# Merge-ring gates and squares, two early buffers, and no address offsets in a one-layer hybrid trunk kernel

## The chip, the cores and the metric

The kernel runs on one core of a Trainium2 chip. The metric is the device time in microseconds (us) of one execution; the time before is the median of three runs, 871.64 us (871.51 to 872.29). In the texts PE is the matrix engine, DVE the vector engine, ACT the scalar engine, POOL the general engine, and SP the engine that only issues transfers. A line number such as L142 is a line of the kernel before.

## The reference

One layer, 512 tokens, 1024 channels, float32. The input is normalised and projected once to 8192 columns, which are split among three token mixers and the gates of three branches:

```python
h = rms_norm(x, norm_mix[l])
proj = jnp.einsum('bsd,dc->bsc', h, w_in[l])
u_pool, u_lru, q, k, v, g_logits = jnp.split(proj, splits, axis=-1)
gates = jax.nn.sigmoid(g_logits + b_gate[l]).reshape(B, S, N_BRANCH, D_MODEL)
y_pool = pool_mixer(u_pool, w_pool[l], pool_scale[l])      # windows 2, 4, 8, 16: mean minus token, 4 maps of 256 x 256
y_lru = rglru_mixer(u_lru, ...)                            # conv of width 4, two gates, decay a, h = a h + b over the tokens
qh, kh = rms_norm(q), rms_norm(k)                          # per head, 8 heads of 128
y_sb = stick_breaking_attention(qh, kh, vh)                # w = sigmoid(z) * prod of (1 - sigmoid) of later keys
merged = sum(gates[:, :, n] * (y_n @ w_branch[n]))         # n = pool, lru, attention
x = x + merged @ w_out
x = x + (silu(h2 @ w_ffn_gate) * (h2 @ w_ffn_up)) @ w_ffn_down     # h2 = rms_norm(x), width 2816
```

## The kernel before

Every large product is made in a split form: each float32 operand is written as a rounded part `hi` and a remainder `lo` (type fp32r), and three matmuls (hi hi, hi lo, lo hi) are accumulated. A weight set of 128 x 1024 is loaded into a tile `raw` or `qw`, ACT copies it to `whi` (L141) and DVE subtracts to `wlo` (L142); 24 or 48 matmuls then use the pair. The pool `wp` holds three of each. The rings are what the text calls sets of equal buffers that tiles take in turn: `mp` has four buffers of 2 x 512 float32 per partition, the ring `b` of the pool `ap0` has 13 of them, and in the attention stage the rings `s` and `l` (`slot`, `slot_ld`) have 30 and 12 buffers of 512 float32. A tile that takes a buffer waits until the last reader of the previous tile in it is done.

The order of the work is set by the program and a planner. The main program walks through weight sets and calls `tick()` between pieces of matmul work; each `tick` emits one entry of a background list (`bg`, and `abg` for attention). Pieces under `tc.high_priority(n)` are moved forward in the order of their engine's queue by the planner, which works with its own costs; the queue that results is fixed when the program is built, and each engine then runs its queue in that order, waiting on semaphores.

The stages, with the times of the profiled execution:

- to about 98 us: `hu`, the scaled input, branch 0's gates (`ps_gate`), the norm, the first LRU chunks `ps_lru`. The matrix engine runs nine warm-up matmuls ahead of the first load.
- about 50 to 130 us: the recurrent mixer, four channel chunks c. `lru_chunk` gives closures: `conv` (L642, L651, twelve steps on DVE, output `xc`), `split` (`xch` L656, `xcl` L657), `gates` (matmuls `lg` L667, then tanh `lr` L671 and `li` L672 on ACT), `tanh` (`li` L676, `lt` L679). Then `lru_exp` (L697, L700), `lru_decay` and `lru_input` (`lt`, `ls`, L705 to L714), and `lru_scan` (L720). Branch 1's gates are computed between these chunks: `gate_store` writes the tanh to `gt` (L609) and a POOL transfer carries it to a scratch tensor.
- about 130 to 290 us: V, K and Q by a seven-product scheme (`ps_q`, L837). A partial result is copied from PSUM by `snap` (`r`, L850) at raised priority, finished by `final` (L854), and `post` makes the squares `sq` (L797) whose sums normalise q and k; `post2` scales K (L816). Then two gate chunks `gx`, `gy`.
- about 290 to 475 us: four pooling chunks (`ps_pool`), then branch 1 of the merge (`ps_br` with `yHH`, `yHL`), then branch 0 (with `yph`, `ypl`). `evac_u` copies a pooling chunk from PSUM (`up`, L983), `pool_mean` makes the window sums on DVE (`pw`, L991, L992, L997) and its split (`p30h`, `p30l` and so on, L941, L942), `pool_back` multiplies by the group's map (`pps`) and writes `yph` (L1010) and `ypl` (L1011). Between half weight sets, a `tick` of `abg` emits the attention pieces of `head_tasks`: loads of q, k, v (`at`, L1052), transposes (`pq`, L1059) and their splits `qkh`, `qkl`, the scores `z`, the scans `E` (L1096), `A` (L1098), transposes of the weights (`pw` on PE, L1109; `wth`, `wtl`), and the output `py`. The PSUM tiles `pq`, `pw`, `py` and `pps` share the three buffers of the pool `paux`; those of `ps_pool` and `ps_br` share the pool `pmm`.
- from about 475 us: branch 2, the output projection and the feed-forward network, with weights split at L1445, L1446 and L1565.

Two things in the tile pools carry no data: `pad`, 41 float32 that shift later tiles of `cst`, and 128 unused columns in each tile of `whi` and `wlo`; a weight tile is the slice that starts at column 0, 4, 8 or 12 (the list `STEPS`, for the first four of some stages) or 16 (`OFF`).

Of the kernel before, what the change touches and what calls it, by code (L numbers as in the profile page):

```python
# [16 lines left out]
P = 128  # L17
# [14 lines left out]
NTICK = (1, 1)  # L32
H = S // 2
AHEAD = 200
PAD = 41


OFF = 16
STEPS = (0, 4, 8, 12)
NAW, NAT, NAB = 8, 8, 13  # L40
NSP = 42
NLD = 12
# [25 lines left out]
def layer_kernel(ctx: ExitStack, tc: tile.TileContext, x, xt, vecs, w_in, w_qkv7, w_gate7, w_pool, w_rg, w_ig,  # L68
# [5 lines left out]
    cst = ctx.enter_context(tc.tile_pool(name="cst", bufs=1))  # L74
    mp = ctx.enter_context(tc.tile_pool(name="mp", bufs=4))
    wp = ctx.enter_context(tc.tile_pool(name="wp", bufs=3))
    late = ctx.enter_context(ExitStack())
    hstack = ctx.enter_context(ExitStack())
    hp = hstack.enter_context(tc.tile_pool(name="hp", bufs=1, side="right"))
# [47 lines left out]
        return [t[:, 0:2, :], t[:, 2:4, :]]  # L127


    def weight_tiles(nh, nl, o=0):  # L130
        return [wp.tile([P, 1024 + 128], F32R, tag=tag, name=n)[:, o:o + 1024]
                for tag, n in (("whi", nh), ("wlo", nl))]

    def split_w(raw, shape, n, o=0):
        hi, lo = weight_tiles("whi" + n, "wlo" + n, o)
        if len(shape) == 3:
            hi, lo = (t.rearrange("p (a b) -> p a b", a=shape[1]) for t in (hi, lo))
        else:
            hi, lo = (t.rearrange("p (a b c) -> p a b c", a=shape[1], b=shape[2]) for t in (hi, lo))
        with tc.high_priority(60):  # L140
            act(hi, raw, AF.Copy)  # L141
            dve.tensor_tensor(lo, raw, hi.bitcast(F32), ALU.subtract)  # L142
        return hi, lo
# [58 lines left out]
    def add_seven(un, nm, i):  # L202
        u, pieces, shape = UNITS[un]
        last = i == pieces - 1

        def make(n):
            if nm == "S4":
                r = qraw[u, "12", i]
                dve.tensor_tensor(r, r, qraw[u, "S2", i], ALU.add)
            src = qraw[u, {"S1": "21", "S3": "11", "S4": "12"}.get(nm, nm), i]  # L210
            o = 0
            if u >= 3:
                o = goffs.pop(0) if goffs else OFF
            parts = split_w(src, [P] + list(shape), n, o)
            if nm == "11":
                qraw[u, "S2", i] = r = b4(list(shape), f"qs{u}{i}")
                dve.tensor_tensor(r, qraw[u, "21", i], src, ALU.add)
                add = nc.gpsimd.dma_start(src, seven_src(u, "21", i), accum_op=ALU.add)
            if last:
                if un < 3:  # L220
                    seven_load(un + 1, {"S1": ("21",), "S3": ("11",), "S4": ("12",), "22": ("22",)}.get(nm, ()))
                elif un == 3 and nm == "11":
                    with tc.issue_after(add.ins):
                        seven_load(un + 1, ("21", "11"))
                elif un == 3:
                    seven_load(un + 1, {"12": ("12",), "S2": ("22",)}.get(nm, ()))
            return parts
        specs.append((("seven", u, nm, i), make))

    goffs = list(STEPS)  # L230

    def add_then(f):
        specs[-1] = (specs[-1][0], lambda n, make=specs[-1][1]: (make(n), f())[0])
# [24 lines left out]
              (0, "S4"), (1, "S2"), (0, "22"), (1, "12"), (1, "S4"), (1, "S3"), (1, "22"))  # L258
    BY, BX = {}, {}
    BNEXT = {"11": ("21", BY), "S1": ("11", BX), "S2": ("12", BX)}  # L260
    boffs = list(STEPS)

    def bsrc(u, nm):
        return w_br7[u, CH[nm], KH[nm]]
# [1 line left out]
    def add_branch7(u, nm):  # L266
        def make(n):
            if nm in ("12", "22"):
                t = wp.tile([P, 2, 4, P], F32, tag="raw", name="raw" + n)
                nc.sync.dma_start(t, bsrc(u, nm))  # L270
            else:
                t = (BY if nm in ("11", "S3") else BX)[u]
            parts = split_w(t, [P, 2, 4, P], n, boffs.pop(0) if boffs else OFF)
            if nm in BNEXT:
                m, buf = BNEXT[nm]
                nc.gpsimd.dma_start(buf[u], bsrc(u, m), accum_op=ALU.add)
            return parts
        specs.append((("b7", u, nm), make))
# [51 lines left out]
        return vt[:, o:o + 1]  # L330


    cst.tile([P, PAD], F32, tag="pad", name="pad")
    warm = cst.tile([P, S], BF16, tag="warm", name="warm")
    dve.memset(warm, 1.0)
    idn = cst.tile([P, P], F32, tag="idn", name="idn")
    make_identity(nc, idn)
# [106 lines left out]
    with ExitStack() as first:  # L444
# [10 lines left out]

        wps = pb.tile([P, 2, S], F32, tag="mm", name="warm_ps")
        for i in range(WARM):
            nc.tensor.matmul(wps[:, 0, :], warm[:, 0:P], warm, start=True, stop=True)

# [137 lines left out]


        def gate_store(br, c, pss, scaled):
            gt = b4([2, S], f"gt{br}{c}")
            for j in range(2):
                o = two(gt[:, j, :])
                g = in_order(pss[j])
                if not scaled:
                    dve.tensor_tensor(o, g, two(rb), ALU.mult)
                    g = o
                act(o, g, AF.Tanh, scale=0.5, bias=bhalf[:, 8 * br + 2 * c + j:8 * br + 2 * c + j + 1])  # L609
            nc.gpsimd.dma_start(gd[br, c].rearrange("(j p) t -> p j t", p=P), gt)  # L610
# [141 lines left out]
        pss.append(chan_chunk(("gate", 0, 3), hu, 2, pb))  # L752
        gate_store(0, 3, pss[3], False)
        tick(len(bg))

        def gate1(c):
            gate_store(1, c, chan_chunk(("gate", 1, c), hn, 1, pb), True)
# [21 lines left out]
        gate1(2)  # L779
        for f, c in ((lru_decay, 2), (lru_decay, 3), (lru_input, 2)):  # L780
            step(of(f, c))
        bg.extend(prepare_t())
        gate1(3)


# [6 lines left out]

        def post(t, i, j, r):
            if t < 2:
                sq = b4([2, 512], f"sq{t}{i}{j}")
                if t == 0:
                    act(sq, r, AF.Square)  # L797
                    dve.tensor_reduce(qss[:, 2 * j:2 * j + 2, 4 * i:4 * i + 4],
                                      sq.rearrange("p a (b d) -> p a b d", d=HD), AX.X, ALU.add)
                    store(t, i, j, r)  # L800
                    return
                s_ = cst.tile([P, 8], F32, tag="ssq", name=f"ssq{t}{i}{j}", bufs=2)
                act(sq, r, AF.Square)
# [88 lines left out]
            nc.gpsimd.dma_start(gd2[cc, j], t)  # L892

        for cc in range(2):
            tx, ty = b4([2, S], f"gx{cc}"), b4([2, S], f"gy{cc}")
            if cc:

                dve.memset(pb.tile([P, 2, S], F32, tag="mm", name="skip_g")[:, 0, 0:1], 0.0)
# [46 lines left out]
    with ExitStack() as mix:  # L945
# [32 lines left out]
                dve.tensor_tensor(lo, r, hi.bitcast(F32), ALU.subtract)  # L978
                pool_w[2 * h + g] = (hi, lo)

        def evac_u(ps, name):
            u = slot(name)
            act(two(u), in_order(ps), AF.Copy)  # L983
            return u

        def pool_mean(g, j, u):
# [32 lines left out]

        def pool_chunk(g):  # L1020
            pss = chan_chunk(("pool", g), hn, 1)
            us = [evac_u(pss[j], f"up{g}{j}") for j in range(2)]
            for j in range(2):
                bg.append(lambda j=j, u=us[j]: pool_mean(g, j, u))
            if g != POOL[0]:
                queue_pool_back(POOL[POOL.index(g) - 1])
# [17 lines left out]
        def head_tasks(h):  # L1044
# [3 lines left out]

            def load():
                for t in range(3):  # L1050
                    r = slot_ld(f"at{h}{t}", (NS, HD))
                    nc.sync.dma_start(r, qd[t, g][:, hd].rearrange("(b p) c -> p b c", p=P))  # L1052
                    st["raw", t] = r

            def trans():
# [117 lines left out]
        def queue_attention():  # L1173
# [8 lines left out]
            for p in range(max(todo) + 1):  # L1182
                abg.append(lambda fs=todo.get(p, ()): [f() for f in fs])

        load_pool_weights(0)
        queue_attention()
        for g in POOL:
            pool_chunk(g)
        queue_pool_back(POOL[3])
# [108 lines left out]
    with ExitStack() as ffn:  # L1298
# [112 lines left out]
        raw = {}  # L1411
        A = {}
        made = [0, NDIRECT]
        offs = []

        def load_a(c):
            for nm in ("11", "21", "22", "12"):
# [11 lines left out]
        def make_a(upto):  # L1429
            while made[0] < min(upto, len(steps)):  # L1430
                c, nm = steps[made[0]]
                made[0] += 1
                if (c, nm) == (NDIRECT, "11"):
                    offs.extend(STEPS)
                while made[1] < min(c + 2, DOWN):
                    load_a(made[1])
                    made[1] += 1
                sums_a(c, nm)
                A[c, nm] = split_a(raw[c, nm], f"{c}_{nm}")

        def split_a(src, n):
            o = offs.pop(0) if offs else OFF
            h, l = (t.rearrange("p (w k c) -> p w k c", w=2, k=4)
                    for t in weight_tiles("wh" + n, "wl" + n, o))
# [134 lines left out]
        def make_d(upto):  # L1579
            while dmade[0] < min(upto, len(dsets)):  # L1580
                nm, n = dsets[dmade[0]]
                dmade[0] += 1
                if dmade[0] == 1:
                    offs.extend(STEPS)
# [157 lines left out]
```

## Time and profile before

| | us |
|---|---|
| median of three runs | 871.64 |
| profiled execution | 872.32 |
| its span | 870.5 |
| PE busy | 860.6 |
| DVE busy | 741.1 |
| ACT busy | 523.1 |
| POOL busy | 91.2 |

The span is what the profiler's records cover; 1.8 us of the profiled execution lie around it. A row of the timeline has the start, the duration, the engine, the line, the operation, output and inputs with their shapes, and in brackets the idle time ahead of it with what ended it. Durations of neighbours on DVE and ACT overlap by about 0.1 us, so that the distance of two starts says what one instruction costs its queue (a split on DVE: 1.22 long, 1.14 from start to start).

### The profile page before, as it was taken

Reading aid. Unit: us, or ns where it says so; the run is one execution under the profiler, and the core shown is the slowest. Engines: PE = TensorE matmul, PEld = TensorE weight load, DVE = VectorE, ACT = ScalarE, POOL = GpSimd, SP = SyncE. Lnnn points to the kernel's source line nnn. Section 1 sums busy time; section 2 is a strip of 40 time slices with the busy share of each in tenths; the row PEclk is TensorE's granted clock in tenths of the full one; section 3 lists DMA queues with packets and bytes.
Section 4 is the critical chain, followed back from the end, with each engine's and each line's share of the span. In section 5 each row is a group of like instructions: output and inputs, shape, how many; then the busy total and the mean of one; then the engine's idle time right before and its main releaser. Section 6 shows DMA issues by size and latency. Waiting matters only on the chain.

```text
span 870.5 us, 14271 instructions
## 1 busy us (share of the span) xinstructions
PE 860.6 (99%) x5563; PEld 790.0 (91%) x5563; DVE 741.1 (85%) x961; ACT 523.1 (60%) x727; POOL 91.2 (10%) x130
## 2 busy tenths in 40 slices
PE   9999999999999999999999999999999999999998
PEld 7888878888899888889889998889999999999998
DVE  7899897998796599977988786699998888899974
ACT  7554989557966565565665545464555555755642
POOL 1110002232433101000001100000000000121200
PEclk9999999999999999999999999999999999999999
DMA  9586356798582886644636955345543433797913
GB/s 339 165 287 203 98 167 187 212 324 253 178 275 73 241 243 203 221 122 151 214 103 167 199 172 169 98 139 151 156 111 97 116 104 119 228 240 194 196 42 121
DMA packets 116643, 154.08 MB, mean 177 GB/s; under 512 B 8160, under 2 KB 90080, under 8 KB 116576
## 3 DMA queue, kind: packets, MB, share of 16 engines
q1 hardware_dynamic: 103904, 107.30, 38.4%
q0 software_dynamic: 12528, 45.62, 22.0%
q8 instruction: 43, 0.70, 0.3%
q10 hardware_dynamic: 144, 0.26, 0.1%
q14 instruction: 24, 0.20, 0.1%
HBM read 132.71 MB, written 18.87 MB: 174 GB/s over the span
## 4 chain that ended last, share of the span: by engine, by line
PE 84%; DVE 7%; ACT 5%; DMA 2%; issue 1%; SPq 0%; ACTq 0%; DVEq 0%
PE ps_y L321 11%; PE ps_x L321 8%; PE ps_q L837 7%; PE ps_dy L1661 6%; PE ps_dx L1661 5%; PE ps_br L312 3%; PE ps_br L313 3%; PE ps_br L314 3%; PE ps_bY L1280 2%; PE ps_gate L740 2%; PE ps_gy L321 2%; DVE wlo L142 2%; PE ps_bX L1280 2%; PE ps_gx L321 2%; PE ps_lru L312 1%; PE ps_out L312 1%
## 5 line engine op out<-in xcount | busy, mean ns | idle before, releaser
L141 ACT ACTIVATE whi<-raw 128x1024 fp32r<-128x1024 f32 x69 | 72.9, 1056 | 78.3 <-PE ps_out L313 16.1
L142 DVE TENSOR_TENSOR wlo<-raw,whi 128x1024 fp32r<-128x1024 f32 x69 | 84.3, 1221 | 24.8 <-ACT whi L141 24.3
L142 DVE TENSOR_TENSOR wlo<-qw,whi 128x1024 fp32r<-128x1024 f32 x48 | 58.4, 1220 | 16.5 <-ACT whi L141 16.3
L141 ACT ACTIVATE whi<-qw 128x1024 fp32r<-128x1024 f32 x48 | 50.6, 1054 | 28.8 <-PE ps_q L837 14.8
L1445 ACT ACTIVATE wh_S<-w_S 128x1024 fp32r<-128x1024 f32 x36 | 38.2, 1062 | 30.2 <-PE ps_y L321 18.3
L1565 POOL DMA_DIRECT2D dw<-in_w_down_dram x20 | 17.0, 864 | 306.1 <-DMA dw<-in_w_down_dram 263.8
L1446 DVE TENSOR_TENSOR wl_S<-w_S,wh_S 128x1024 fp32r<-128x1024 f32 x36 | 43.9, 1221 | 3.2 <-ACT wh_S L1445 3.2
L1445 ACT ACTIVATE wh<-w 128x1024 fp32r<-128x1024 f32 x27 | 28.6, 1060 | 29.3 <-PE ps_x L321 9.1
L1446 DVE TENSOR_TENSOR wl<-w,wh 128x1024 fp32r<-128x1024 f32 x27 | 33.0, 1221 | 8.2 <-ACT wh L1445 8.2
L1445 ACT ACTIVATE whdS<-dw 128x1024 fp32r<-128x1024 f32 x20 | 21.2, 1061 | 20.3 <-PE ps_dy L1661 11.2
L1096 DVE TENSOR_TENSOR_SCAN E<-K,ahead 128x512 f32<-128x512 f32 (+3 forms) x32 | 25.4, 814 | 3.9 <-ACT K L1092 3.9
L1446 DVE TENSOR_TENSOR wldS<-dw,whdS 128x1024 fp32r<-128x1024 f32 x20 | 24.2, 1222 | 4.9 <-ACT whdS L1445 4.9
L312 PE MATMUL ps_br<-yHH,whi 128*128 128x512 f32 x64 | 24.6, 385 | 1.4 <-ACT up L983 1.4
L312 PE MATMUL ps_lru<-HH,whi 128*128 128x512 f32 x64 | 24.6, 384 | 0.0
L312 PE MATMUL ps_br<-yph,whi 128*128 128x512 f32 x64 | 24.5, 383 | 0.0
L312 PE MATMUL ps_pool<-HH,whi 128*128 128x512 f32 x64 | 24.5, 383 | 0.0
L312 PE MATMUL ps_gate<-HH,whi 128*128 128x512 f32 x64 | 24.4, 381 | 0.0
L313 PE MATMUL ps_lru<-HL,whi 128*128 128x512 f32 x64 | 24.3, 379 | 0.0
L314 PE MATMUL ps_lru<-HH,wlo 128*128 128x512 f32 x64 | 24.3, 379 | 0.0
L313 PE MATMUL ps_gate<-HL,whi 128*128 128x512 f32 x64 | 24.3, 379 | 0.0
L314 PE MATMUL ps_gate<-HH,wlo 128*128 128x512 f32 x64 | 24.3, 379 | 0.0
L313 PE MATMUL ps_pool<-HL,whi 128*128 128x512 f32 x64 | 24.3, 379 | 0.0
(740 smaller groups left out, 3444.5 us busy)
## 6 DMA issues: line engine op xcount, KB each, us to landing
raw<-in_w_in_dram SPq DMA_DIRECT2D x31, 512.0 KB, 5.3
qw<-in_w_qkv_dram SPq DMA_DIRECT2D x24, 512.0 KB, 6.8
dw<-in_w_down_dram POOLq DMA_DIRECT2D x20, 512.0 KB, 9.2
w<-in_w_ffn_gate_dram SPq DMA_DIRECT2D x36, 256.0 KB, 3.7
w<-in_w_ffn_up_dram SPq DMA_DIRECT2D x36, 256.0 KB, 4.2
raw<-in_w_branch_dram SPq DMA_DIRECT2D x16, 512.0 KB, 3.9
qw<-in_w_qkv_dram POOLq DMA_DIRECT2D x12, 512.0 KB, 8.1
qd<-r POOLq DMA_DIRECT2D x12, 512.0 KB, 6.7
```

The lines of the kernel that those rows point to most:

```text
L141: act(hi, raw, AF.Copy)
L142: dve.tensor_tensor(lo, raw, hi.bitcast(F32), ALU.subtract)
L312: nc.tensor.matmul(ps, lh, rh, start=start, stop=False, skip_group_check=skip)
L313: nc.tensor.matmul(ps, lh, rl, start=False, stop=False, skip_group_check=skip)
L314: nc.tensor.matmul(ps, ll, rh, start=False, stop=stop, skip_group_check=skip)
L321: nc.tensor.matmul(o, a_[a][:, w, k, :], il2(b_[b][:, k, :]), start=first and n == k == 0, stop=last and n == 2 and k == 3, skip_group_che ...
L837: nc.tensor.matmul(ps[:, a, :], b_[:, k, ts_], il(a_[:, kk, :]), start=first and n == k == 0, stop=n == 2 and k == 3, skip_group_check=True)
L1096: dve.tensor_tensor_scan(E[:, c0:c0 + n][:, ::-1], K[:, c0 + 1:c0 + n + 1][:, ::-1], ahead[:, S - n:][:, ::-1], 0.0, ALU.mult, ALU.add)
L1280: nc.tensor.matmul(o, ah[x_][:, w, k, :], il2(b[k][y_]), start=first_ and n == k == 0, stop=n == 2 and k == 3, skip_group_check=True)
L1445: act(h, src, AF.Copy)
L1446: dve.tensor_tensor(l, src, h.bitcast(F32), ALU.subtract)
L1661: nc.tensor.matmul(o, a_[a][:, w, k0 + k, :], il2(b_[b][:, k, :]), start=first and i == k == 0, stop=last and i == 2 and k == nk - 1, skip ...
```

## The change

The gate tiles of branch 1 (`gt10` to `gt13`) and the squares `sq` take the four buffers of `mp`, which the merge uses later, in place of buffers of the ring `b`. The tiles `gx`, `gy` of the two gate chunks take `b` and `w` rings. The entries of `prepare_t` are run right after branch 0's last gate is emitted, not queued later. A new pool `ex` has two buffers of 512 float32. The first head's q and k loads (`at00`, `at01`) take them, under raised priority; when these are done, the last pooling chunk's copies (`up20`, `up21`: the last in the order of `POOL`) take them, also under raised priority. The attention list is built ahead of the pooling chunks, and its first entry, the loads of head 0, is emitted at once, ahead of the pooling weights. The offsets and pads of weight tiles and of `cst` are gone, and the warm-up tile has 128 columns that are read four times over.

```diff
+    ex = ctx.enter_context(tc.tile_pool(name="ex", bufs=2))
...
-    def weight_tiles(nh, nl, o=0):
-        return [wp.tile([P, 1024 + 128], F32R, tag=tag, name=n)[:, o:o + 1024]
+    def weight_tiles(nh, nl):
+        return [wp.tile([P, 1024], F32R, tag=tag, name=n)
...
-    cst.tile([P, PAD], F32, tag="pad", name="pad")
-    warm = cst.tile([P, S], BF16, tag="warm", name="warm")
+    warm = cst.tile([P, P], BF16, tag="warm", name="warm")
...
-            nc.tensor.matmul(wps[:, 0, :], warm[:, 0:P], warm, start=True, stop=True)
+            nc.tensor.matmul(wps[:, 0, :], warm, warm.unsqueeze(1).to_broadcast([P, 4, P]), start=True, stop=True)
...
-            gt = b4([2, S], f"gt{br}{c}")
+            gt = mp.tile([P, 2, S], F32, tag="m", name=f"gt{br}{c}") if br else b4([2, S], f"gt{br}{c}")
...
         tick(len(bg))
+        for f in prepare_t():
+            f()
...
-        bg.extend(prepare_t())
         gate1(3)
...
-                sq = b4([2, 512], f"sq{t}{i}{j}")
+                sq = mp.tile([P, 2, 512], F32, tag="m", name=f"sq{t}{i}{j}")
...
-            tx, ty = b4([2, S], f"gx{cc}"), b4([2, S], f"gy{cc}")
+            tx, ty = (b4([2, S], f"g{n}{cc}", "bw"[cc]) for n in "xy")
...
-        def evac_u(ps, name):
-            u = slot(name)
-            act(two(u), in_order(ps), AF.Copy)
+        def evac_u(ps, name, last):
+            u = ex.tile([P, S], F32, tag="u", name=name) if last else slot(name)
+            with tc.high_priority(EARLY if last else 0):
+                act(two(u), in_order(ps), AF.Copy)
             return u
...
-            us = [evac_u(pss[j], f"up{g}{j}") for j in range(2)]
+            us = [evac_u(pss[j], f"up{g}{j}", g == POOL[3]) for j in range(2)]
...
                 for t in range(3):
-                    r = slot_ld(f"at{h}{t}", (NS, HD))
-                    nc.sync.dma_start(r, qd[t, g][:, hd].rearrange("(b p) c -> p b c", p=P))
+                    with tc.high_priority(400 if h == 0 and t < 2 else 0):
+                        r = (ex.tile([P, NS, HD], F32, tag="u", name=f"at{h}{t}") if h == 0 and t < 2
+                             else slot_ld(f"at{h}{t}", (NS, HD)))
+                        nc.sync.dma_start(r, qd[t, g][:, hd].rearrange("(b p) c -> p b c", p=P))
...
-        load_pool_weights(0)
         queue_attention()
+        abg.pop(0)()
+        load_pool_weights(0)
```

More of the change, by code (lines that the diff above doesn't have):

```diff
@@ L34 @@
 AHEAD = 200
-PAD = 41
-OFF = 16
-STEPS = (0, 4, 8, 12)
 NAW, NAT, NAB = 8, 8, 13
@@ L127, in halves, with split_w @@
         return [t[:, 0:2, :], t[:, 2:4, :]]
-    def weight_tiles(nh, nl, o=0):
-        return [wp.tile([P, 1024 + 128], F32R, tag=tag, name=n)[:, o:o + 1024]
+    def weight_tiles(nh, nl):
+        return [wp.tile([P, 1024], F32R, tag=tag, name=n)
                 for tag, n in (("whi", nh), ("wlo", nl))]
-    def split_w(raw, shape, n, o=0):
-        hi, lo = weight_tiles("whi" + n, "wlo" + n, o)
+    def split_w(raw, shape, n):
+        hi, lo = weight_tiles("whi" + n, "wlo" + n)
         if len(shape) == 3:
@@ L210, in make @@
             src = qraw[u, {"S1": "21", "S3": "11", "S4": "12"}.get(nm, nm), i]
[L211 to L214, printed above, removed]
+            parts = split_w(src, [P] + list(shape), n)
             if nm == "11":
@@ L228, in add_seven @@
         specs.append((("seven", u, nm, i), make))
-    goffs = list(STEPS)
     def add_then(f):
@@ L260, in layer_kernel @@
     BNEXT = {"11": ("21", BY), "S1": ("11", BX), "S2": ("12", BX)}
-    boffs = list(STEPS)
     def bsrc(u, nm):
@@ L272, in make @@
                 t = (BY if nm in ("11", "S3") else BX)[u]
-            parts = split_w(t, [P, 2, 4, P], n, boffs.pop(0) if boffs else OFF)
+            parts = split_w(t, [P, 2, 4, P], n)
             if nm in BNEXT:
@@ L1183, in queue_attention @@
                 abg.append(lambda fs=todo.get(p, ()): [f() for f in fs])
+        queue_attention()
+        abg.pop(0)()
         load_pool_weights(0)
-        queue_attention()
         for g in POOL:
@@ L1413, in layer_kernel @@
         made = [0, NDIRECT]
-        offs = []
         def load_a(c):
@@ L1432, in make_a @@
                 made[0] += 1
-                if (c, nm) == (NDIRECT, "11"):
-                    offs.extend(STEPS)
                 while made[1] < min(c + 2, DOWN):
@@ L1441, in split_a @@
         def split_a(src, n):
-            o = offs.pop(0) if offs else OFF
             h, l = (t.rearrange("p (w k c) -> p w k c", w=2, k=4)
-                    for t in weight_tiles("wh" + n, "wl" + n, o))
+                    for t in weight_tiles("wh" + n, "wl" + n))
             act(h, src, AF.Copy)
@@ L1582, in make_d @@
                 dmade[0] += 1
-                if dmade[0] == 1:
-                    offs.extend(STEPS)
                 dfetch(dmade[0])
```

## The prediction

> **What bounds the kernel now.** I read the page's busy lines first, then the waits of TensorE (PE), then the timeline around each wait, since only work that releases PE late can move this kernel.
>
> ```profile
> PE 860.6 (99%) x5563; PEld 790.0 (91%) x5563; DVE 741.1 (85%) x961; ACT 523.1 (60%) x727; POOL 91.2 (10%) x130
> DVE  7899897998796599977988786699998888899974
> ```
>
> PE is busy for 99% of the span. The second line is DVE (VectorE) in tenths, in 40 slices of 21.8 us: the 15th to the 17th (305 to 370 us) are all 9, so its queue has little slack to give there.
>
> ```profile
> PE warm_ps L458 <- DVE warm L335: 1.5, 1, 1.5
> PE ps_br L312 <- ACT up L983: 1.4, 1, 1.4
> PE lg L667 <- DVE xcl L657: 1.4, 1, 1.4
> PE ps_q L837 <- DVE wlo L142: 1.2, 3, 0.7
> ...
> PE pq L1059 <- DVE wtl L1112: 0.2, 1, 0.2
> ```
>
> Columns: who waits, for what, us in total, times, longest. The view has nine rows, falling from 1.5 to 0.2; the four between those shown are at most 1.2 each, so all nine lie between 6.5 and 10.5 us of 870.5, and the first is the start, which the change leaves alone. Little can be won, while every engine that is put behind can lose more. The profiled execution took 872.32 us (span 870.5 and 1.8 around it), 0.68 above the median of 871.64; the sum below is made on 872.32 and then lowered by 0.68.
>
> **The change part by part.** Eight edits: (1) branch 1's gate tiles and (2) the squares move from the large pool's ring to the merge ring; (3) transposing preparation is issued earlier in the source; (4) `gx`/`gy` take other rings; (5) the first head's q and k loads and (6) the last pooling copies take a new ring `ex`, with raised priority; (7) the attention queue is set up ahead of the pool chunks and its first task is run at once; (8) pads, offsets and the wide warm tile go.
>
> (3), (4), (8): The order of every engine is the same up to 94 us, so (3) moves nothing there; (4) moves nothing that I can find. For (8), the durations of the split, in ns (minimum, median, maximum), with their first and last start:
>
> ```profile
> L142 DVE TENSOR_TENSOR wlo<-raw,whi x69: 1200/1221/1228, 9.7 to 761.1; 128x1024 fp32r<-128x1024 f32 x69
> L142 DVE TENSOR_TENSOR wlo<-bw,whi x10: 1216/1226/1227, 461.2 to 500.5; 128x1024 fp32r<-128x1024 f32 x10
> ```
>
> The second group holds offset tiles (0, 4, 8, 12 in turn, then 16): minimum 1216, maximum 1227 ns. I take 0. With 127 splits and a spread of 11 ns the bounds are -1.4 and +1.4 us if every split were on the path; nearly none is.
>
> (1), gates of branch 1. A gate tile no longer waits for a buffer of the large ring, so the gate's tanh stands ahead of the recurrence's tanhs on ACT (ScalarE), and the planner puts the split `whi` of the weight set numbered 21 behind all four of `lr`, `li` that followed it.
>
> ```profile
> 113.03 1.06 ACT L141 ACTIVATE whi<-raw 128x1024 fp32r<-128x1024 f32 x1
> 113.99 0.67 ACT L671 ACTIVATE lr<-lg,brg 64x512 f32<-64x512 f32 x1
> ...
> 116.78 1.06 ACT L141 ACTIVATE whi<-raw 128x1024 fp32r<-128x1024 f32 x1
> ...
> 114.12 1.23 DVE L142 TENSOR_TENSOR wlo<-raw,whi 128x1024 fp32r<-128x1024 f32 x1 [0.29 <-ACT whi L141]
> 115.26 3.33 DVE L651 SCALAR_TENSOR_TENSOR xc<-ps_lru,vt,xc 128x1 f32<-128x1 f32 x9
> 118.51 1.21 DVE L142 TENSOR_TENSOR wlo<-raw,whi 128x1024 fp32r<-128x1024 f32 x1
> ...
> 121.38 1.22 DVE L657 TENSOR_TENSOR xcl<-xc,xch 128x1024 fp32r<-128x1024 f32 x1
> 122.65 0.72 PE lg L667 x4
> 98.04 0.23 PE ps_lru L313
> ```
>
> In the new order `whi` 21 starts where the fourth tanh ends. The four take 113.99 to 116.78, 2.8 us; the ACT work ahead of them stands 0.45 earlier, because of work moved behind: `whi` 21 from 115.4 to 116.4 instead of 113.03 to 114.09. The next DVE instruction, its `wlo`, waits for it, and everything on DVE behind that waits too: the `wlo` 1.14 by starts (114.12 to 115.26), the rest of the convolution (two more of its steps go ahead, seven of nine are left: 2.5 of the 3.25 from 115.26 to 118.51), and the block of the next `wlo`, `xch`, `li` and `xcl`, 4.09 from 118.51 to 122.60: 116.45 + 7.73 = 124.2, against 122.60 before. PE starts `lg` at 122.65 as `xcl` ends, so +1.6. Bounds: 0, if the planner's displaced convolution steps fill the wait, and 2.33, the whole delay of `whi` 21.
>
> [...]
>
> The recurrence is also planned in another place behind this. Weight set 32 is split behind two scans now, and behind four in the new order:
>
> ```profile
> 158.87 2.33 DVE L720 TENSOR_TENSOR_SCAN li<-lt,ls 128x512 f32<-128x512 f32 x2
> 161.12 1.20 DVE L142 TENSOR_TENSOR wlo<-qw,whi 128x1024 fp32r<-128x1024 f32 x1
> 162.37 3.72 PE ps_q L837 x16
> ```
>
> PE waits for that `wlo` and starts at 162.37. Two more scans are 2.25 by starts (158.87 to 161.12), and some 0.4 of DVE's lateness is left by then: 162.32 + 2.25 + 0.4 = 165.0. PE is 1.6 late already, so +1.1 here: +2.7 in all by 165 us. Bounds of the 1.1: 0 (DVE has caught up) and 2.25.
>
> (2), squares. The copy of the K partial on ACT now goes ahead of a `whi`:
>
> ```profile
> 234.34 1.01 ACT L850 ACTIVATE r<-ps_q 128x1024 f32<-128x1024 f32 x1
> 234.34 0.38 PE L837 MATMUL ps_q0S<-wlo,hT1h 128*128 128x512 f32 x1
> 234.56 0.38 PE L837 MATMUL ps_q0S<-whi,hT1l 128*128 128x512 f32 x1
> 235.40 0.48 PE L837 MATMUL ps_q<-whi,hT3h 128*128 128x512 f32 x1 [0.46 <-ACT r L850]
> ```
>
> PE's start stands 0.84 behind the matmul at 234.56, where the pitch is 0.22 (234.34 to 234.56): 0.62, and 0.1 more for the longer first matmul (0.48 against 0.38). The copy becomes ready in time: -0.72.
>
> (5), (7), first head. Its loads are issued behind a weight load now and ahead of it after; they have `ex`, not the ring of loaded slots.
>
> ```profile
> 298.70 0.38 PE L314 MATMUL ps_pool<-HH,wlo 128*128 128x512 f32 x1
> 299.12 0.63 PE L1059 MATMUL pq<-idn,at 128*128 128x128 f32 x4
> 299.93 0.66 PE L1059 MATMUL pq<-idn,at 128*128 128x128 f32 x4 [0.18 <-DMA at<-qd]
> 300.34 0.46 PE L312 MATMUL ps_pool<-HH,whi 128*128 128x512 f32 x1
> ```
>
> From 298.70, 0.42 to the first and 0.81 to the second group where the pitch asks 0.22 and 4 x 0.11 (an estimate from the row of `pw` below: ten in 1.26, to the end of the last); with the restart it is 0.61. They land several us sooner: -0.61. The weight load that they go ahead of lands later; what hides that is the weights already split, and if that cover is gone it gives the 0.61 back (bounds -0.61 and 0).
>
> (6), last pooling copies. PE waits for a slot of PSUM that ACT's copy `up` frees:
>
> ```profile
> 347.97 0.38 PE L314 MATMUL ps_br<-yHH,wlo 128*128 128x512 f32 x1
> 349.79 0.48 PE L312 MATMUL ps_br<-yHH,whi 128*128 128x512 f32 x1 [1.44 <-ACT up L983]
> 349.12 1.10 ACT L983 ACTIVATE up<-ps_pool 128x512 f32<-128x512 f32 x2
> 348.11 0.74 DVE L1011 SCALAR_TENSOR_TENSOR ypl<-pps,vt,yph 128x512 fp32r<-128x512 f32 x1
> 352.48 1.26 PE L1109 MATMUL pw<-idn,A 128*128 128x128 f32 x10
> ```
>
> 1.82 less 0.22, and 0.1 to restart: 1.70. The copy no longer waits for a slot that DVE frees, so it can run by 344: -1.70, and some -0.3 from small waits further on.
>
> (7) again: every attention task now comes half a weight chunk, 2.6 us, earlier on PE (12 x 0.216), the pooling work on DVE not. The three auxiliary PSUM slots are shared. In the new order the second `pw` of head 1 takes the slot that `ypl` of pool group 0 frees. That `ypl` ends at 348.85 and `pw` starts at 352.48 now, 3.6 us later. After, a `wlo`, the end of a pooled mean and its split stand ahead of that `ypl` on a saturated DVE: I place its end at 353.2, with `pw` asked for at 351: +1.6 (bounds 0 and 2.3). Likewise a little earlier +0.5 (`pw` of head 0 behind `ypl` of group 1), and at head 2:
>
> ```profile
> 372.16 1.41 DVE L1011 SCALAR_TENSOR_TENSOR ypl<-pps,vt,yph 128x512 fp32r<-128x512 f32 x2
> 374.90 1.26 PE L1109 MATMUL pw<-idn,A 128*128 128x128 f32 x10
> ```
>
> Margin now 2.74 from start to start; asked for 2.6 earlier and with `ypl` later, I take +1.5 (bounds 0 and 2.2: part of the lateness is in PE already).
>
> Sum: +1.6 +1.1 -0.72 -0.61 -1.70 -0.3 +0.5 +1.6 +1.5 = +3.0: 872.32 + 3.0 = 875.3, less 0.68: 874.6 us.
>
> **The rivals.**
> Faster: DVE's lead absorbs the displaced work. Both additions hang on how far DVE is behind PE in two stretches; I walked its queue by hand, and an error of 0.1 us in each of 20 instructions is 2 us. If `xcl` ends by 122.6 and `ypl` of group 0 by 351, only the gains are left: 871.64 - 3.3 = 868.3. For it: the removed waits are certain in the order; against it: `whi` 21 is behind four tanhs in the order, whatever the durations. The point from which it decides: additions under 1.6 in place of 6.3. [...] Chance 0.16.
>
> No difference: the recurrence loses its 2.7, the attention stretch none, for DVE is ready by `pw`: 871.64 + 2.7 - 3.3 = 871.0. For it: the 3.6 of margin. Chance 0.2.
>
> Slower still: all additions at their upper bounds, 2.33 + 2.25 + 0.5 + 2.3 + 2.2 = 9.6, less 3.3: 877.9. Chance 0.1.
>
> The pads do matter: the 1.4 of (8), on top of the forecast or off it, 873.2 to 876.0. Chance 0.04.
>
> **How the numbers follow.** Forecast 874.6, chance 0.5, own range 873.0 to 876.5. About 0.2% (1.7 us: 869.9 and 873.4) is what a measurement tells from no change. Faster: the first rival, 0.16. Same: 0.2 and 0.04 of the forecast's lower edge, 0.24. Slower: the rest, 0.6. The range 869.0 to 877.5 leaves out the far half of the first and of the third rival, under 0.2.
>
> **What would show it.** Right: the `lg` wait for `xcl` near 3 us, the wait for `wlo` at 162 near 1.9, no wait of `ps_br` for `up` nor of `pq` for `at`, new waits of `pw` for `ypl`. Wrong: `lg` at 1.4 or less, `pw` without waits, or a `wlo` group whose mean differs by over 11 ns.

## The result and the profile after

The changed kernel takes 881.16 us (median of six runs, 878.94 to 883.78), the kernel before 871.58 in the same comparison: the ratio is 1.0108, with a 95% interval of 1.0091 to 1.0126. The direction was forecast; the size was three times the 3.0 us of the sum, and the time lies above the range. The runs of the changed kernel spread over 4.8 us, those of before over 1.3. The profiled run is the slowest of the six, 883.78 us, with a span of 882.0. The granted clock, as a mean over each run, is 0.994 in the profiled one, 0.997 in the fastest (878.94), 0.998 and 0.996 in two more (880.92 and 881.43), and 1.000 in the other two, which took 880.20 and 881.40.

The busy lines and the line of the granted clock, from the page of the changed kernel:

```profile
PE 865.0 (98%) x5563; PEld 792.7 (90%) x5563; DVE 741.9 (84%) x961; ACT 521.9 (59%) x727; POOL 90.9 (10%) x130
PEclk9999989999999999999999999999999999999999
```

DVE and ACT do the same work as before (741.1 and 523.1 us). PE's own busy time is longer by 4.4 us, and the sixth slice of the clock (110 to 132 us) is not full. The second thing is new: before, the clock line was 9 throughout.

The waits of PE in the changed kernel (who waits, for what, us in total, times, longest):

```profile
PE pw L1104 <- DVE ypl L1004: 4.3, 3, 2.0
PE lg L658 <- DVE xcl L648: 1.7, 1, 1.7
PE ps_q L829 <- DVE wlo L140: 1.5, 2, 1.0
PE ps_gy L313 <- ACT gx L905: 1.3, 1, 1.3
PE pq L1054 <- DVE wtl L1107: 1.1, 1, 1.1
...
PE lg L658 <- DVE xch L647: 1.0, 1, 1.0
```

The waits of `ps_br` for `up` (1.4) and of `pq` for its load are gone, as forecast, and `pw` waits for `ypl`, as forecast too, but 4.3 us and not 3.6. The two longest of these waits, with the `ypl` that ends the first:

```profile
357.38 0.75 DVE L1004 SCALAR_TENSOR_TENSOR ypl<-pps,vt,yph 128x512 fp32r<-128x512 f32 x1
358.27 0.52 PE L1104 MATMUL pw<-idn,A 128*128 128x128 f32 x3 [1.95 <-DVE ypl L1004]
382.01 0.55 PE L1104 MATMUL pw<-idn,A 128*128 128x128 f32 x3 [1.67 <-DVE ypl L1004]
```

Three waits were not in the sum: `ps_gy` for `gx`, `pq` for `wtl` (1.1, before 0.2), and one of the two for `wlo`, which stands at 229 us.

Where the recurrence is worked (timeline of the changed kernel: start, duration, engine, line, operation, tiles, idle time before):

```profile
114.35 0.68 ACT L663 ACTIVATE li<-lg,bigx 64x512 f32<-64x512 f32 x1
115.05 2.02 ACT L139 ACTIVATE whi<-raw 128x1024 fp32r<-128x1024 f32 x2
...
116.14 1.23 DVE L140 TENSOR_TENSOR wlo<-raw,whi 128x1024 fp32r<-128x1024 f32 x1 [1.19 <-ACT whi L139]
117.28 2.56 DVE L642 SCALAR_TENSOR_TENSOR xc<-ps_lru,vt,xc 128x2 f32<-128x2 f32 x7
...
121.72 0.48 PE L658 MATMUL lg<-xch,lwh 64*128 64x512 f32 x2 [0.97 <-DVE xch L647]
123.90 0.79 PE L658 MATMUL lg<-xcl,lwh 64*128 64x512 f32 x2 [1.70 <-DVE xcl L648]
```

`whi` 21 starts at 115.05 behind the fourth tanh (forecast 115.4), DVE waits 1.19 us for it, with steps of the convolution behind it in its queue, and PE gets `xcl` at 123.90 (forecast 124.2). And then something that no step of the prediction had: the same matmuls take twice as long (0.43 us from start to start at 127 us, 0.22 at 119). The table by stretches shows it (length, then busy time and count of PE, PEld, DVE, ACT and POOL, then the granted clock, the transfer share and GB/s):

```profile
122.00:124.00 2.00, 0.30 (x4) 0.10 (x2) 2.00 (x3) 0.00 (x0) 0.00 (x0) 0.88 0.08 17
124.00:126.00 2.00, 2.00 (x10) 1.41 (x10) 1.97 (x2) 0.82 (x2) 0.00 (x0) 0.50 0.75 245
128.00:130.00 2.00, 2.00 (x6) 1.55 (x6) 0.47 (x1) 1.98 (x3) 0.00 (x0) 0.50 0.98 395
130.00:132.00 2.00, 2.00 (x10) 1.72 (x9) 1.22 (x2) 1.95 (x4) 0.00 (x0) 0.92 0.93 317
360.00:362.00 2.00, 2.00 (x6) 1.53 (x6) 2.00 (x4) 1.68 (x4) 0.00 (x0) 0.50 0.30 104
```

After 2.7 us of waiting in two pieces the granted clock is 0.50 until 130.3 us. Matched matmul by matmul with the kernel before, PE's lateness (how much later the same matmul starts) grows from 1.25 us at `xcl` to 4.36 us in that stretch. A second one, from 359.0 to 362.4 us, stands behind the wait of `pw` at 358 us; against gt_back below, which has the same matmuls there at full speed, it costs 1.6. So 4.7 of the 11.5 us by which the two profiled spans differ were lost at half speed behind waits when they were lost. What remains of them at the end is less: PE that is late by a stretch waits less later on. And the two runs with a clock of 1.000 lost 8.6 and 9.8 us without any such stretch.

### The profile page after: what moved, and what is told of

Its sections match the earlier page's. It is cut to its first block, busy times and chain, and to the rows that moved or that the text cites. A ratio compares the mean times of both kernels' runs of the same rounds, so it can differ in the third digit from the quotient of the medians.

```text
span 882.0 us, 14272 instructions
## 1 busy us (share of the span) xinstructions
PE 865.0 (98%) x5563; PEld 792.7 (90%) x5563; DVE 741.9 (84%) x961; ACT 521.9 (59%) x727; POOL 90.9 (10%) x130
## 4 chain that ended last, share of the span: by engine, by line
PE 54%; DVE 6%; ACT 1%; issue 1%; DMA 1%; ACTq 0%; DVEq 0%; SPq 0%
PE ps_y L313 11%; PE ps_x L313 8%; PE ps_dy L1651 5%; PE ps_dx L1651 4%; PE ps_br L306 2%; PE ps_br L305 2%; PE ps_bY L1276 2%; PE ps_br L304 2%; PE ps_bX L1276 2%; PE ps_out L304 1%; PE ps_out L305 1%; PE ps_out L306 1%; PE ps_fu L305 1%; PE ps_fu L304 1%; PE ps_fu L306 1%
## 5 line engine op out<-in xcount | busy, mean ns | idle before, releaser
L306 PE MATMUL ps_br<-yHH,wlo 128*128 128x512 f32 x64 | 25.2, 393 | 0.0
L305 PE MATMUL ps_br<-yHL,whi 128*128 128x512 f32 x64 | 24.8, 388 | 0.0
L305 PE MATMUL ps_br<-ypl,whi 128*128 128x512 f32 x64 | 24.3, 380 | 0.0
```

Of the source, the lines that this page charges most:

```text
L305: nc.tensor.matmul(ps, lh, rl, start=False, stop=False, skip_group_check=skip)
L306: nc.tensor.matmul(ps, ll, rh, start=False, stop=stop, skip_group_check=skip)
```

## The experiments

**One part undone.** Two theories stood against each other: that the order of the queues (and the clock behind it) costs the time, part by part, or that the removed pads and offsets do. Four kernels tell them apart.

Edit (8) alone on the kernel before:

```diff
-        return [wp.tile([P, 1024 + 128], F32R, tag=tag, name=n)[:, o:o + 1024]
+        return [wp.tile([P, 1024], F32R, tag=tag, name=n)
...
-    cst.tile([P, PAD], F32, tag="pad", name="pad")
-    warm = cst.tile([P, S], BF16, tag="warm", name="warm")
+    warm = cst.tile([P, P], BF16, tag="warm", name="warm")
```

> The kernel before with edit (8) alone: no pads, no offsets, narrow warm-up tile; every engine's order is as before. Theory A: 871.6 us, within 0.5 of the kernel before, and no half-clock stretch. Theory B (pads): 874 us or more, with longer splits on DVE or a wider pitch on PE.

Measured: 871.51 us, ratio 0.9997 (0.9988 to 1.0007). The pads are out, in either direction, to within 0.1%, and this kernel is the base for the ones that add a single part.

The phase of the attention list put back, all else as changed:

```diff
         abg.pop(0)()
+        abg.insert(0, lambda: None)
         load_pool_weights(0)
```

> Only the phase of edit (7) undone: one empty entry stands behind the first head's loads in the attention list, so that every later piece comes half a weight chunk later again, as before; the early loads and the buffers of ex stay. Theory A (phase against the pooling work on DVE): the waits of pw for ypl (4.3 us) and the half-clock stretch near 360 us go, and the two gains of this stage stay (pq for at 0.6, ps_br for up 1.7): 881.2 - 4.3 - 1 = 876 us. Theory B (the pooling copies' new buffers and priority push DVE and ACT work late): the waits of pw for ypl stay at 3 us or more, 880 us.

Measured: 875.67 us (874.82 to 878.51), ratio 1.0053 (1.0035 to 1.0071). All three waits of `pw` are gone; by the two ratios the phase alone costs 0.55%, 4.8 us, half of the loss. The largest waits that are left:

```profile
PE ps_q L829 <- DVE wlo L140: 2.1, 2, 1.1
PE lg L658 <- DVE xcl L648: 1.7, 1, 1.7
PE pq L1054 <- DVE wtl L1107: 1.3, 2, 1.1
...
PE lg L658 <- DVE xch L647: 1.0, 1, 1.0
```

The gates of branch 1 put back to the large ring, all else as changed:

```diff
-            gt = mp.tile([P, 2, S], F32, tag="m", name=f"gt{br}{c}") if br else b4([2, S], f"gt{br}{c}")
+            gt = b4([2, S], f"gt{br}{c}")
```

> Edit (1) alone undone in the changed kernel: branch 1's gate tiles go back to the large ring. In the queue order the weight copy whi 21 then stands between the recurrence's tanhs again. Theory A (order and clock): PE's waits for xch and xcl near 122 us shrink from 3.2 to 1.7 us, the half-clock stretch after them (6.7 us at half speed in the changed kernel's profile) does not occur there, the three waits for wlo between 145 and 163 come back (0.4, 0.4, 0.8): 878.5 us. Theory B (the pads and addresses, not the order, cost the time): within 0.5 us of the changed kernel, 881.

Measured: 879.31 us (876.37 to 881.19), ratio 1.0086 (1.0065 to 1.0108). `xcl` is waited for 1.4 us again, `xch` not at all, and the three waits for `wlo` are back. The profiled run has a recorded clock of 1.0 throughout, though `pw` waits 4.2 us in it. It is also late from its start: eight of its first matmuls, up to 9.3 us, have a pitch of 0.43 us in place of 0.216 (in the kernel before one, at 6.0), and it is 2.0 us behind by 16 us. The spread of 4.8 us is as wide as before, so the time itself says little; the next set measures edit (1) from the other side.

The squares put back, all else as changed:

```diff
-                sq = mp.tile([P, 2, 512], F32, tag="m", name=f"sq{t}{i}{j}")
+                sq = b4([2, 512], f"sq{t}{i}{j}")
```

> Edit (2) alone undone: the squares go back to the large ring. Theory A: the two new waits of PE that stand at 229 us (wlo, 1.3 us) and 262 us (the copy gx behind a square on ACT, 1.4 us) go, the old one at 235 us (the partial's copy r, 0.6 us) comes back: 2.1 us less than the changed kernel, 879.0 us. Theory B (pads): 881. If the 262 us wait stays, the new rings of gx and gy make it, not the squares.

Measured: 879.5 us (878.83 to 881.76), ratio 1.0097 (1.008 to 1.0114). The waits at 229 and 262 us went and the one at 235 came back. This run shows a second thing by chance: it waits for `xch` and `xcl` as long as the changed kernel, but the clock does not halve there, and then the wait for `wlo` at 165 us is 1.6 us long (changed kernel: 0.67 lost there).

```profile
PE pw L1104 <- DVE ypl L1004: 3.9, 3, 2.0
PE ps_q L829 <- DVE wlo L140: 1.9, 2, 1.6
PE lg L658 <- DVE xcl L648: 1.7, 1, 1.7
```

The half-clock stretch thus had hidden a wait that the prediction had right: PE that is late by other means no longer waits.

**One part alone.** On the base without pads, edit (1) alone:

```diff
-            gt = b4([2, S], f"gt{br}{c}")
+            gt = mp.tile([P, 2, S], F32, tag="m", name=f"gt{br}{c}") if br else b4([2, S], f"gt{br}{c}")
```

> The kernel before without pads and with edit (1) alone. Theory A: the waits for xch and xcl near 122 us are 3.2 us in place of 1.7, and in some executions the clock halves behind them: 873 us when it does not, up to 876 when it does, no other new wait. Theory B (edit (1) hurts only together with the others): 871.6 us.

Measured: 885.23 us, ratio 1.0153 (1.0139 to 1.0167): both theories miss. The longest wait of PE, and ACT's timeline at the place:

```profile
PE ps_q L836 <- ACT whi L141: 12.2, 1, 12.2
```

```profile
144.86 1.06 ACT L708 ACTIVATE lt<-lt 128x1024 f32<-128x1024 f32 x1 [0.41 <-DVE lt L704]
152.60 0.69 ACT L608 ACTIVATE gt<-ps_gate,bhalf 128x512 f32<-128x512 f32 x1 [6.68 <-DMA gd<-gt]
153.18 1.01 ACT L849 ACTIVATE r<-ps_q 128x1024 f32<-128x1024 f32 x1
```

The merge ring's four buffers also hold the four differences `hT` that edit (3)'s preparation makes. With the old place of the preparation, the fourth gate tile waits 6.7 us until a transfer has emptied a buffer, and the weight splits stand in ACT's queue behind it. So the two edits were run together on the same base:

```diff
         tick(len(bg))
+        for f in prepare_t():
+            f()
...
-        bg.extend(prepare_t())
...
-            gt = b4([2, S], f"gt{br}{c}")
+            gt = mp.tile([P, 2, S], F32, tag="m", name=f"gt{br}{c}") if br else b4([2, S], f"gt{br}{c}")
```

> The kernel before without pads, with edits (1) and (3) alone: branch 1's gates in merge buffers and the preparation of the token products emitted early. Theory A (edit (3) only removes the 12 us wait that edit (1) alone makes): the recurrence's waits as in the changed kernel, 3.2 us near 122, and 1.8 at 165 if the clock does not halve or 0.7 if it does: 871.6 + 2.4 = 874.0 us, up to 875 in executions with a half-clock stretch. Theory B (edit (3) moves nothing): 885 us as gt_only.

Measured: 874.48 us (873.29 to 875.6), ratio 1.0034 (1.0022 to 1.0046): +3.0, the price of edits (1) and (3) as a pair. The waits are those of the changed kernel (`xcl` 1.7, `xch` 1.0), and in the profile a half-clock stretch of 3.4 us follows them. I had expected up to 875 us with such a stretch and less without; the three runs with a clock of 0.998 took 873.63, 874.65 and 874.97, the three with 1.000 took 873.29, 874.31 and 875.60.

Edit (2) alone on the base without pads:

```diff
-                sq = b4([2, 512], f"sq{t}{i}{j}")
+                sq = mp.tile([P, 2, 512], F32, tag="m", name=f"sq{t}{i}{j}")
```

> The kernel before without pads, with edit (2) alone: all squares in merge buffers. Theory A (the late sum of squares on DVE makes the K scale, and with it a weight split, late): +1.2 us for a wait for wlo near 225 us, -0.7 for the copy at 235 us: 871.6 + 0.5 = 872.1 us. Theory B (that wait comes with the recurrence's lateness only): 870.9 us.

Measured: 873.22 us, ratio 1.0020 (1.0011 to 1.0029): +1.7, above both theories, which lacked the wait for `gx`. DVE's timeline shows where it comes from (the K chain), and the waits of PE show both losses:

```profile
213.29 1.22 DVE L142 TENSOR_TENSOR wlo<-qw,whi 128x1024 fp32r<-128x1024 f32 x1
216.05 0.17 DVE L349 TENSOR_TENSOR krs<-rsqq 128x8 f32<-128x8 f32 x1 [1.54 <-POOL rsqq L348]
```

```profile
PE ps_q L836 <- DVE wlo L142: 2.4, 5, 1.0
...
PE ps_gy L321 <- ACT gx L912: 0.7, 1, 0.7
```

The sum of squares `ssq111` is planned behind two more instructions on DVE (2.3 us), POOL makes its inverse root later, and `krs11`, which stands in DVE's queue at a fixed place, holds the whole queue 1.54 us for it. PE then waits for a `wlo` near 226 us. And the square `sq010` now stands ahead of `gx0` on ACT and waits for its own input, so `gx0` is late: 0.7 here, 1.3 in the changed kernel's profile, none in the profiles of gt_back and phase_back, in which ACT's order there is the same. So its size varies; what sets it is not shown.

The phase back, and edits (1) and (2) undone: what is left are the early loads (5), the buffers and priority of the last pooling copies (6), the rings of `gx` and `gy` (4), the early preparation (3), and no pads.

```diff
-            gt = mp.tile([P, 2, S], F32, tag="m", name=f"gt{br}{c}") if br else b4([2, S], f"gt{br}{c}")
+            gt = b4([2, S], f"gt{br}{c}")
...
-                sq = mp.tile([P, 2, 512], F32, tag="m", name=f"sq{t}{i}{j}")
+                sq = b4([2, 512], f"sq{t}{i}{j}")
...
         abg.pop(0)()
+        abg.insert(0, lambda: None)
```

> The changed kernel with edits (1) and (2) undone and the phase put back: left are the first head's early loads, the pooling copies' own buffers and priority, the gx and gy rings and no pads. Theory A (the parts' effects add): 871.6 - 0.6 (pq for at) - 1.7 (ps_br for up) + 1.3 (the pq wait for wtl near 360 us, if it stays) = 870.6 us; without that wait 869.3. Theory B (the copies' priority pushes other ACT work late): 872 us or more, with waits of pw or pq for DVE of 2 us and more.

Then the same without edit (6):

```diff
-            u = ex.tile([P, S], F32, tag="u", name=name) if last else slot(name)
-            with tc.high_priority(EARLY if last else 0):
+            u = slot(name)
+            with tc.high_priority(0):
```

> As early_bufs, but the last pooling copies keep their slots of the large ring and their old priority: only the first head's loads are early. Theory A: the wait of ps_br for up near 349 us is back (1.7 us), the wait of pq for wtl near 360 us is as in the kernel before (none over 0.4): 871.6 - 0.6 = 871.0 us. Theory B (the load that the early loads pass is late and holds PE up): 872 us or more, with a wait of PE for a weight set near 300 us.

Measured: early_bufs 871.49 us, ratio 0.9997 (0.9988 to 1.0006), between the two theories; early_loads 870.86 us, ratio 0.9986 (0.9978 to 0.9995). The early loads gain what was forecast (871.51 - 870.86 = 0.65 between the medians; 0.11%, 0.96 us, between the ratios). Edit (6) gains nothing and costs 0.6 (871.49 - 870.86, medians of eleven runs each, measured side by side): the wait of `ps_br` for `up` goes, and in the profile of early_bufs another one of 1.5 us stands some 7 us later:

```profile
356.05 1.12 PE L1054 MATMUL pq<-idn,at 128*128 128x128 f32 x8 [1.52 <-DVE wtl L1107]
```

```profile
354.17 1.22 DVE L140 TENSOR_TENSOR wlo<-raw,whi 128x1024 fp32r<-128x1024 f32 x1
355.31 1.62 DVE L1107 TENSOR_TENSOR wtl<-pw,wth 128x512 fp32r<-128x512 f32 x3
```

DVE runs without a gap there; PE, no longer held at 349, comes sooner to DVE's next result.

**The clock by itself.** Why did the clock halve behind some waits and not behind others? Two kernels without the layer run bursts of matmuls with idle times between them that ACT makes (a chain of copies from the burst's result to the next burst's operand):

```python
for tp, chain in CASES:                      # the second kernel
    for rep in range(REPS):
        if tp:                               # ten 128x128 transposes ahead of the idle time
            ...
        src = ps
        for wd in chain:                     # copies of 128, 256 or 512 columns
            act(tt[:, 0:wd], src[:, 0:wd], AF.Copy, scale=1e-3 if src is ps else 1.0)
            src = tt
        act(rs[cur], src, AF.Copy)
        ps = burst(rs[cur], 58 + 5 * ((g * 7) % 4) + (g % 3), f"b{g}")
```

> This kernel leaves the layer out: it copies x to its output and runs 65 bursts of 58 to 75 matmuls of 128x512 (13 to 16 us each), with idle times of PE between them that ACT makes, from about 1 to 4 us in eight lengths, four times each; in the second half ten 128x128 transposes stand ahead of each idle time. It measures when the granted clock halves. [...] Theory B (transposes count as idle too): in the second half the halving begins at an idle time 1.1 us shorter. [...]

> As gap_micro (the layer is left out), with the transposes bound behind each burst, and shorter idle times: four lengths from about 0.9 to 2.1 us without transposes, five from 0.9 to 2.9 us behind ten transposes, six times each. Theory A (only the idle counts): no half-clock stretch under 1.9 us in either half. Theory B (ten transposes, 1.1 us, count as idle): in the second half stretches begin at an idle of 0.9 to 1.6 us.

In the first kernel the transposes of the second half were planned ahead of the bursts, so that half has hardly any idle time and says nothing; in the second kernel they are bound behind the burst. The idle times, counted from the last matmul's start and its pitch (0.216 us, a transpose 0.11) to the start of the next burst, and how many of them were followed by matmuls at 0.43 us:

| idle, us | without transposes | idle, us | behind ten transposes |
|---|---|---|---|
| 0.92, 1.37, 1.58 | 0 of 20 | 0.91, 1.57 | 0 of 12 |
| 1.92 | 0 of 6 | 2.02 | 2 of 6 |
| 2.03 | 2 of 4 | 2.24 | 3 of 6 |
| 2.24, 2.69, 2.90 | 9 of 12 | 2.68 | 4 of 6 |
| 3.35, 3.56 | 4 of 8 | | |
| 4.22 | 4 of 4 | | |

By the starts of the matmuls, a stretch was 3.4 to 3.75 us long and cost 1.7 to 1.8, or 5.7 to 6.1 us and cost 2.9 to 3.1; the record of the granted clock gives 3.41 and 6.83 us, of which a part can lie in the idle time. Two idle times of the second kernel that are alike in length, with and without a stretch behind them (timeline rows, whose brackets count from the modelled end of the last matmul and so give 0.17 less than the table above; then the table by stretches, in which the clock stands ahead of the transfer share):

```profile
634.40 5.76 PE L93 MATMUL b<-r,w 128*128 128x512 f32 x17 [1.85 <-ACT r L109]
...
656.04 6.19 PE L93 MATMUL b<-r,w 128*128 128x512 f32 x26 [1.86 <-ACT r L109]
```

```profile
634.40:639.50 5.10, 5.10 (x15) 4.05 (x16) 0.00 (x0) 0.00 (x0) 0.67 0.00 0
656.00:661.00 5.00, 4.96 (x22) 4.11 (x23) 0.00 (x0) 0.00 (x0) 1.00 0.00 0
```

So in these two kernels an idle time of PE of 2.02 us and more cost up to 3.1 us at once in some cases; one of up to 1.92 us without transposes never did, in 26 cases. Measured in the same way, from the starts of the matmuls, the longest idle times of the kernel before are 1.73 and 1.60 us, both shorter than 1.92, and no stretch follows them; the changed kernel's are 1.13 and 2.07 nearly in a row, 2.1 and 1.9, and the first pair and the 2.1 were followed by a stretch in its profile, the 1.9 was not. That transposes count as idle with their whole 1.1 us did not show: six idle times of about 1.57 us behind ten transposes brought nothing.

What decides between two idle times of the same length is not shown. In the changed kernel's profile the record has the clock at 0.50 from 123.50 to 130.33 and from 359.02 to 362.44 us: the first begins inside the wait for `xcl`, which ends at 123.90, the second 0.75 us behind the end of the wait of `pw`. In sq_back, which waited as long for `xch` and `xcl` (1.0 and 1.7), the clock stayed full there.

What a stretch costs in the end is less than it takes. Up to 167 us, behind the wait for `wlo`, PE's lateness from the recurrence is 2.4 us in sq_back (no stretch there), 2.3 in gt_prep and 2.4 in phase_back (a stretch of 3.4 us, which takes 1.6), and 3.3 in the changed kernel (6.8 us, which takes 3.1). Set against gt_back, the second stretch takes 1.6 us in the changed kernel and 1.7 in sq_back, and 1.3 and 1.4 are left behind the next wait of `pw`. So 2.3 us of the profiled run's 11.5 remain from its two stretches.

**A version that gains.** The early loads, and of all squares only the first of Q in a merge buffer:

```diff
-                sq = b4([2, 512], f"sq{t}{i}{j}")
+                sq = (mp.tile([P, 2, 512], F32, tag="m", name=f"sq{t}{i}{j}") if t == 0 and (i, j) == (0, 0) else
+                      b4([2, 512], f"sq{t}{i}{j}"))
```

> early_loads with one more edit: the first square of Q alone (sq000) takes a merge buffer, so that the copy r001 goes ahead of a weight copy on ACT, while the squares of K and the last ones of Q keep the large ring. Theory A (each square's place costs or gains by itself): the 235 us wait (0.7) goes, no wait at 229 or 262 us comes: 870.9 - 0.7 = 870.2 us. Theory B (any move of a square delays the K chain on DVE): a wait for wlo near 225 us of 1 us, 871.3 us or more.

Measured: 870.01 us (median of eleven), ratio 0.9984 (0.9975 to 0.9992). The wait at 235 us is gone and no new one has come; the five longest that are left:

```profile
PE ps_br L304 <- ACT up L977: 1.4, 1, 1.4
PE lg L658 <- DVE xcl L648: 1.4, 1, 1.4
PE ps_q L830 <- DVE wlo L140: 1.1, 3, 0.7
PE warm_ps L449 <- DVE warm L326: 1.1, 1, 1.1
PE z L305 <- DVE qkl L1059: 0.3, 1, 0.3
```

It beats both kernels, by 1.5 and 11 us; the gain over the kernel before is 0.16%. Ten of its eleven runs lie within 0.6 us, and one stands at 872.77.

## Why the prediction was wrong, point by point

By the lateness of the same matmuls in the profiles (us), the sum went wrong in two of its three places:

| stage | forecast | changed kernel | without a stretch there |
|---|---|---|---|
| recurrence, to 167 us | +2.7 | +3.3 | +2.4 (sq_back) |
| K, Q and squares, 167 to 290 us | -0.7 | +2.4 | +1.2 (gt_back) |
| pooling and first heads, 290 to 470 us | +1.0 | +5.9 | +3.5 (gt_back) |

The right column adds up to 7.1 in place of 3.0, with the clock full.

- Edit (8), taken at 0: right (0.9997).
- Edit (1), +1.6 and +1.1: the place, the cause and nearly the size were right (+2.4 for the two without a stretch). The pair of edits (1) and (3) costs 3.0. That the steps of the convolution behind `wlo` wait with it shows in the changed kernel: DVE idles 1.19 us ahead of the `wlo` at 116.14 with seven steps behind it, though the last `ps_lru` matmul ends at 105.2 us. Without a half-clock stretch the wait at 165 us is 1.8 us lost by the starts of the matmuls (sq_back), forecast 1.9.
- Edit (3), "moves nothing there": true of the order up to 94 us, but no step said that edit (1) needs it. Without it PE waits 12.2 us, because the merge ring has other users. I had priced the ring that the gates left and not the one that they joined.
- Edit (2), -0.72: this is the first step that failed. The copy at 235 us did become ready in time, and in the profile of loads_sq0 that wait is gone with no other in its place (in time this last gain is small: 0.85 us between its median and that of early_loads, but only 0.02% between their ratios, since the kernel before was itself 0.56 faster in the later comparison). But the sum looked at ACT's order alone and gave nothing for the sums of squares that change place in DVE's, nor for what waits for them: the chain over POOL to `krs`, which holds DVE. With it and `gx`, the edit costs 1.7, where -0.72 was forecast.
- Edit (5), -0.61: right (0.65 to 0.96).
- Edit (6), -1.70: failed. The wait went, as forecast, but the sum did not ask what is late next once this wait is gone. DVE was late next, and in early_bufs the gain of 1.70 became a loss of 0.6.
- Edit (7), +0.5, +1.6, +1.5: right in place and mechanism (0.84, 2.1 and 1.9 us by the starts of the matmuls), 1.2 us too small. I had lowered the third term since PE would be late already; it was not, since the same DVE queue sets both. A wait of `pq` for `wtl` at 442 us (1.1) was missing as well. By the ratios the phase costs 4.8; in the profiles the lateness from 290 to 470 us grows by 3.5 in gt_back, which has no stretch, and by nothing in phase_back.
- The clock: a term that is missing altogether, but not the one that makes the forecast fail. Every wait in the sum was priced at its length, and in the profile before, whose longest idle time is 1.73 us, nothing showed otherwise. In the profiled run the two stretches took 4.7 us and left 2.3; two of the six runs had none and were still 5.6 and 6.8 us above the forecast of 874.6. Over the single runs the clock does not order the times: no difference shows in gt_prep, and in gt_back there are 3 us between the mean of two runs with a stretch and that of two without.

The measured parts add up: +0.34% (1 and 3), +0.20% (2), +0.55% (7), -0.03% (8, 5 and 6 together with 3 and 4, by early_bufs) make 1.06%, against 1.08% measured. The rival "slower still" (877.9) had the right sign, and `pw` did wait longer than forecast, but it too lacked `krs`, DVE's next result and the clock; the rival "Faster", by which only the gains are left, held for the loads alone.

## What to carry to other kernels

A wait of the matrix engine can be dearer than it is long: here, behind a wait of 2.1 us and behind two of 1.13 and 2.07 us nearly in a row, half-clock stretches of 3.41 and 6.83 us followed, which took 1.6 and 3.1 us. A forecast with such waits needs a term for it, but a small one where more waits follow: 0 to 1.4 us remained of each stretch. When tiles move to another ring of buffers, list the users of the ring that they join and every queue position that the planner changes, and follow each changed position to whoever waits for it, small instructions too (here 12.2 us for a gate tile in the joined ring, and 1.54 us of DVE for one `krs`). And an engine that runs without a gap hands a removed wait on (here the 1.4 us of `ps_br` for `up` came back as 1.5 us of `pq` for `wtl`): at such a place a gain counts only after the next result of that engine has been checked.

## What was not expected of the hardware

The halving behind waits of little over 2 us; that sq_back waited as long for `xch` and `xcl` (1.0 and 1.7 us) as the changed kernel and kept its full clock there; and that a stretch which takes 1.6 or 3.1 us can leave nothing or 0.9 behind the next wait. The runs of the changed kernel spread over 4.8 us, and those of the versions without a wait of 1.9 us over 0.9 and 0.8 (early_loads, early_bufs). The clock does not explain that spread by itself: the fastest run of the changed kernel had a clock of 0.997, and the two with 1.000 lie 1.2 us apart. The late `gx` (0 to 1.3 us) and the start (2.0 us in gt_back) vary too; how much each gives is not shown.
